# Splitting a GpSimd product in two: one product over an interleaved signed-sine table against two half products over a sine table and a negative-sine table

## The chip, the cores and the metric

One core of one Trainium2 chip runs the program. The metric is the device time of one execution in microseconds (us). Lower is better. Most executions of one kernel agree within 0.3%. Some are slower, and runs over 1.5% above the fastest of the same kernel are called slow and left out of comparisons. Faster or slower needs 2%.

## The reference

```python
# x: (8, 2048, 8, 64) float32; cos, sin: (2048, 32) float32
x1, x2 = x[..., :32], x[..., 32:]
out1 = x1 * cos - x2 * sin
out2 = x1 * sin + x2 * cos
return np.concatenate([out1, out2], axis=-1)      # cos, sin broadcast over batch and head
```

33.5 MB come in and 33.5 MB go out. Per output element there are two products and one sum.

## The kernel before

A batch is one tile of 128 partitions and 8192 elements (4 MB). Five such buffers rotate. Each batch is worked in tiles of mostly 2048 elements (sometimes 1024), in one of three ways: A puts t1 = x times cosine on the vector engine (DVE), t2 = swapped x times signed sine on GpSimd (POOL) and the sum on DVE. B is the same with the sum on the tensor engine and the copy-out on ACT (the scalar engine). C uses no GpSimd. Of the 34 tiles 32 are of kind A or B.

```python
cos_sb = t1s_pool.tile([P, R, Dh], f32, tag="t1s", name="cos_sb")
sin_sb = t1s_pool.tile([P, R, Dh], f32, tag="t1s", name="sin_sb")
sgn = const_pool.tile([P, R, 2, Dh], f32, tag="sg")      # -sin and sin, interleaved
# ... cut ...
for lo, hi in ((0, 4), (4, R)):                          # lines 90 and 91, on ACT
    keep(nc.scalar.mul(sgn[:, lo:hi, 0, :], sin_sb[:, lo:hi, :], -1.0))
    keep(nc.scalar.copy(sgn[:, lo:hi, 1, :], sin_sb[:, lo:hi, :]))
# ... cut: in rotate(), for kinds A and B ...
keep(nc.gpsimd.tensor_mul(                               # line 134
    out=t2.rearrange("p (r h u d) -> p r h u d", r=nr, h=H, u=2),
    in0=swapped(xt, nr),                                 # halves of each head exchanged, negative step
    in1=signed(sgn[:, r0 : r0 + nr, :, :], nr)))
keep(nc.vector.tensor_mul(out=t1..., in0=xk, in1=rep(cos_ps[...], 2 * H)))   # line 141
if kind == "A":
    keep(nc.vector.tensor_add(out=xt, in0=t1, in1=t2))   # line 148
# ... cut: kinds B and C; store() on the ACT queue is line 74, load() on the SP queue line 67 ...
```

Of the kernel before, what the change touches and what calls it, by code (L numbers as in the profile page):

```python
# [9 lines left out]
@with_exitstack  # L10
def kernel(
    ctx: ExitStack,
    tc: tile.TileContext,
    x: bass.AP,
    cos: bass.AP,
    sin: bass.AP,
    out: bass.AP,
):
    nc = tc.nc
    keep = tc.keep_in_program_order  # L20
    f32 = mybir.dt.float32
    PSUM = bass.MemoryType.PSUM

    B, S, H, D = x.shape
    Dh = D // 2
    P = 128
    HD = H * D
    R = S // P
    ROW = R * HD
    UNIT = 4 * HD  # L30
    NBUF = 5
    C = 512
    last = B - 1

    xv = x.rearrange("b (q r) h d -> b q (r h d)", q=P)
    ov = out.rearrange("b (q r) h d -> b q (r h d)", q=P)
    cos_src = cos.rearrange("(q r) d -> q r d", q=P)
    sin_src = sin.rearrange("(q r) d -> q r d", q=P)

    const_pool = ctx.enter_context(tc.tile_pool(name="const", bufs=1))  # L40
    tab_pool = ctx.enter_context(tc.tile_pool(name="tab", bufs=1, space=PSUM))
    t1_pool = ctx.enter_context(tc.tile_pool(name="t1p", bufs=1, space=PSUM))
    o_pool = ctx.enter_context(tc.tile_pool(name="op", bufs=2, space=PSUM))
    t1s_pool = ctx.enter_context(tc.tile_pool(name="t1s", bufs=2))
    xpool = ctx.enter_context(tc.tile_pool(name="xpool", bufs=NBUF))
    t2_pool = ctx.enter_context(tc.tile_pool(name="t2p", bufs=3))

    cos_sb = t1s_pool.tile([P, R, Dh], f32, tag="t1s", name="cos_sb")
    sin_sb = t1s_pool.tile([P, R, Dh], f32, tag="t1s", name="sin_sb")
    sgn = const_pool.tile([P, R, 2, Dh], f32, tag="sg")  # L50
    eye = const_pool.tile([P, P], f32, tag="eye")
    neye = const_pool.tile([P, P], f32, tag="neye")
    cos_ps = tab_pool.tile([P, R, Dh], f32, tag="cp")
    sin_ps = tab_pool.tile([P, R, Dh], f32, tag="sp")

    xts = {}

    def spans(sizes):
        lo = 0
        for n in sizes:  # L60
            yield lo, n
            lo += n

    def load(b):
        xt = xpool.tile([P, ROW], f32, tag="xt", name=f"xt{b}")
        for lo, n in spans([UNIT, UNIT, 2 * UNIT] if b == 0 else [ROW]):
            keep(nc.sync.dma_start(out=xt[:, lo : lo + n], in_=xv[b, :, lo : lo + n]))  # L67
            if b == 0 and lo == 0:
                keep(nc.sync.dma_start(out=cos_sb, in_=cos_src))  # L69
                keep(nc.sync.dma_start(out=sin_sb, in_=sin_src))  # L70
        xts[b] = xt

    def store(b, lo, n):
        keep(nc.scalar.dma_start(out=ov[b, :, lo : lo + n], in_=xts[b][:, lo : lo + n]))  # L74

    for b in range(NBUF):
        load(b)

    nc.gpsimd.memset(eye, 0.0)  # L79
    nc.gpsimd.affine_select(  # L80
        out=eye,
        in_=eye,
        compare_op=mybir.AluOpType.not_equal,
        fill=1.0,
        base=0,
        pattern=[[-1, P]],
        channel_multiplier=1,
    )
    for lo, hi in ((0, 4), (4, R)):
        keep(nc.scalar.mul(sgn[:, lo:hi, 0, :], sin_sb[:, lo:hi, :], -1.0))  # L90
        keep(nc.scalar.copy(sgn[:, lo:hi, 1, :], sin_sb[:, lo:hi, :]))  # L91
    keep(nc.scalar.copy(sin_ps, sin_sb))  # L92
    keep(nc.scalar.mul(neye, eye, -1.0))
    keep(nc.vector.tensor_copy(cos_ps, cos_sb))  # L94

    def rep(a, n):
        return dataclasses.replace(a, ap=[a.ap[0][:], a.ap[1][:], [0, n], a.ap[-1][:]])

    def swapped(a, nr):
        return dataclasses.replace(  # L100
            a,
            offset=a.offset + Dh,
            ap=[a.ap[0][:], [HD, nr], [D, H], [-Dh, 2], [1, Dh]],
        )

    def signed(a, nr):
        return dataclasses.replace(
            a, ap=[a.ap[0][:], [D, nr], [0, H], [Dh, 2], [1, Dh]]
        )

    kinds = {}
    for b, kind in ((1, "C"), (2, "B"), (3, "C"), (4, "B"), (5, "B")):
        kinds[(b, 0)] = kind

    def rotate(b, lo, n):
        kind = kinds.get((b, lo), "A")
        xt = xts[b][:, lo : lo + n]
        r0 = lo // HD
        nr = n // HD
        xk = xt.rearrange("p (r k d) -> p r k d", r=nr, d=Dh)  # L120
        xu = xt.rearrange("p (g u d) -> p g u d", u=2, d=Dh)
        if kind == "A":
            t1 = t1_pool.tile([P, n], f32, tag="t1")
        else:
            t1 = t1s_pool.tile([P, n], f32, tag="t1s")
        if kind == "C":
            t2 = t1s_pool.tile([P, n], f32, tag="t1s")
        else:
            t2 = t2_pool.tile([P, n], f32, tag="t2")
        t1u = t1.rearrange("p (g u d) -> p g u d", u=2, d=Dh)  # L130
        t2u = t2.rearrange("p (g u d) -> p g u d", u=2, d=Dh)
        if kind != "C":
            keep(
                nc.gpsimd.tensor_mul(  # L134
                    out=t2.rearrange("p (r h u d) -> p r h u d", r=nr, h=H, u=2),
                    in0=swapped(xt, nr),
                    in1=signed(sgn[:, r0 : r0 + nr, :, :], nr),
                )
            )
        keep(  # L140
            nc.vector.tensor_mul(  # L141
                out=t1.rearrange("p (r k d) -> p r k d", r=nr, d=Dh),
                in0=xk,
                in1=rep(cos_ps[:, r0 : r0 + nr, :], 2 * H),
            )
        )
        if kind == "A":
            keep(nc.vector.tensor_add(out=xt, in0=t1, in1=t2))  # L148
        elif kind == "B":
            for j in range(n // C):  # L150
                o = o_pool.tile([P, C], f32, tag="o")
                cs = slice(j * C, (j + 1) * C)
                nc.tensor.matmul(o, eye, t1[:, cs], start=True, stop=False)  # L153
                nc.tensor.matmul(o, eye, t2[:, cs], start=False, stop=True)  # L154
                keep(nc.scalar.copy(xt[:, cs], o))  # L155
        else:
            keep(
                nc.vector.tensor_mul(  # L158
                    out=t2.rearrange("p (r k d) -> p r k d", r=nr, d=Dh),
                    in0=xk,  # L160
                    in1=rep(sin_ps[:, r0 : r0 + nr, :], 2 * H),
                )
            )
            G = C // Dh
            for u in range(2):
                for j in range(n // 2 // C):
                    o = o_pool.tile([P, C], f32, tag="o")
                    gs = slice(j * G, (j + 1) * G)
                    nc.tensor.matmul(o, eye, t1u[:, gs, u, :], start=True, stop=False)  # L169
                    nc.tensor.matmul(  # L170
                        o, eye if u else neye, t2u[:, gs, 1 - u, :], start=False, stop=True
                    )
                    keep(
                        nc.scalar.copy(  # L174
                            xu[:, gs, u, :], o.rearrange("p (g d) -> p g d", d=Dh)
                        )
                    )

    def pieces(b):
        if b == 0:  # L180
            return [2 * HD, 2 * HD, UNIT, UNIT, UNIT]
        if b == last:
            return [UNIT, UNIT, UNIT, 2 * HD, 2 * HD]
        return [UNIT] * 4

    def shares(b):
        if b == 0:
            return [HD, 7 * HD, 2 * UNIT]
        if b == last:
            return [2 * UNIT, UNIT, UNIT]  # L190
        return [ROW]

    for b in range(B):
        done = 0
        outs = list(spans(shares(b)))
        for lo, n in spans(pieces(b)):
            rotate(b, lo, n)
            done = lo + n
            while outs and sum(outs[0]) <= done:
                store(b, *outs.pop(0))  # L200
        if b + NBUF <= last:
            load(b + NBUF)
# [30 lines left out]
```

## Time and profile before

| | before |
|---|---|
| median of the first three runs | 163.64 us (163.49 to 164.29) |
| span in the profile | 161.6 us |
| DVE / GpSimd busy | 87% / 84% |
| share of the two DMA queues | 49.7% + 48.3% |

Two rows of the page's slices (tenths of each of 40 slices that the engine was busy) and the row of the chain that ended last, for the kernel before:

```profile
DVE  0458999999999999999999899999999998999900
...
POOL 1199999999999799989995989997999969999100
...
DMA 46%; DVE 36%; POOL 8%; issue 4%; SPq 1%; ACT 0%; DVEq 0%; POOLq 0%; ACTq 0%
```

Three resources look nearly full. The rows cannot say which of them is the bound. GpSimd's sevens, fives and sixes are pauses in which it waits for a load or for a free buffer.

### The profile page before, as it was taken

Reading aid. Unit: us, or ns where it says so; the run is one execution under the profiler, and the core shown is the slowest. Engines: PE = TensorE matmul, PEld = TensorE weight load, DVE = VectorE, ACT = ScalarE, POOL = GpSimd, SP = SyncE. Lnnn points to the kernel's source line nnn. Section 1 sums busy time; section 2 is a strip of 40 time slices with the busy share of each in tenths; the row PEclk is TensorE's granted clock in tenths of the full one; section 3 lists DMA queues with packets and bytes.
Section 4 is the critical chain, followed back from the end, with each engine's and each line's share of the span. In section 5 each row is a group of like instructions: output and inputs, shape, how many; then the busy total and the mean of one; then the engine's idle time right before and its main releaser. Section 6 shows DMA issues by size and latency. Waiting matters only on the chain.

```text
span 161.6 us, 440 instructions
## 1 busy us (share of the span) xinstructions
PE 47.1 (29%) x80; PEld 18.7 (12%) x80; DVE 140.1 (87%) x66; ACT 15.1 (9%) x27; POOL 135.8 (84%) x38
## 2 busy tenths in 40 slices
PE   0000000499008940895029901991000000000000
PEld 0000000134003410331014301340000000000000
DVE  0458999999999999999999899999999998999900
ACT  3310000012100220022001300121000000000000
POOL 1199999999999799989995989997999969999100
PEclk9999999999855898579556995599755555555555
DMA  5999999899999999999999998999999999999994
GB/s 187 418 438 482 463 397 390 373 426 507 397 389 450 426 487 389 446 462 389 446 462 389 462 448 381 487 422 389 487 422 397 479 422 397 479 422 397 430 400 209
DMA packets 3457, 67.64 MB, mean 419 GB/s; under 512 B 384, under 2 KB 384, under 8 KB 768
## 3 DMA queue, kind: packets, MB, share of 16 engines
q1 hardware_dynamic: 1728, 34.08, 49.7%
q10 hardware_dynamic: 1728, 33.56, 48.3%
q14 instruction: 1, 0.01, 0.0%
HBM read 34.08 MB, written 33.55 MB: 419 GB/s over the span
## 4 chain that ended last, share of the span: by engine, by line
DMA 46%; DVE 36%; POOL 8%; issue 4%; SPq 1%; ACT 0%; DVEq 0%; POOLq 0%; ACTq 0%
DMA xt<-in_x_dram 24%; DVE t L141 19%; DMA out_dram<-xt 18%; DVE xt L148 16%; POOL t L134 8%; DMA sin_sb<-in_sin_dram 3%; DVE t L158 1%; SPq L69 0%; SPq L67 0%; ACT sgn L91 0%; DVEq L148 0%; ACT sgn L90 0%; POOLq L134 0%; ACTq L74 0%
## 5 line engine op out<-in xcount | busy, mean ns | idle before, releaser
L134 POOL TENSOR_TENSOR t<-xt,sgn 128x2048 f32<-128x2048 f32 (+1 forms) x32 | 135.1, 4253 | 13.5 <-ACT sgn L91 6.0
L141 DVE TENSOR_TENSOR t<-xt,cos_ps 128x2048 f32<-128x2048 f32 (+1 forms) x34 | 73.4, 2166 | 0.8
L148 DVE TENSOR_TENSOR xt<-t,t 128x2048 f32<-128x2048 f32 (+1 forms) x29 | 62.2, 2144 | 6.3 <-POOL t L134 3.4
L153 PE MATMUL o<-t,eye 128*128 128x512 f32 x24 | 16.1, 759 | 24.7 <-DVE t L141 24.7
L169 PE MATMUL o<-t,eye 128*128 128x512 f32 x16 | 11.8, 844 | 37.6 <-DVE t L141 37.6
L154 PE MATMUL o<-t,eye 128*128 128x512 f32 x24 | 14.9, 709 | 0.0
L155 ACT COPY xt<-o 128x512 f32<-128x512 f32 x12 | 7.0, 586 | 45.0 <-PE o L154 45.0
L153 PEld LDWEIGHTS o<-t,eye 128*128 128x128 f32 x24 | 5.8, 255 | 33.0 <-issue 33.0
L174 ACT COPY xt<-o 128x512 f32<-128x512 f32 x8 | 4.7, 586 | 44.6 <-DVE t L141 26.0
L169 PEld LDWEIGHTS o<-t,eye 128*128 128x128 f32 x16 | 3.8, 256 | 42.5 <-POOL t L134 30.6
L154 PEld LDWEIGHTS o<-t,eye 128*128 128x128 f32 x24 | 5.4, 227 | 7.8 <-issue 7.8
L94 DVE COPY cos_ps<-cos_sb 128x512 f32<-128x512 f32 x1 | 0.7, 694 | 6.1 <-DMA cos_sb<-in_cos_dram 6.1
L170 PE MATMUL o<-t,neye 128*128 128x512 f32 x8 | 5.7, 830 | 0.2 <-DVE t L158 0.2
L158 DVE TENSOR_TENSOR t<-xt,sin_ps 128x2048 f32<-128x2048 f32 x2 | 4.6, 2279 | 0.0
L170 PE MATMUL o<-t,eye 128*128 128x512 f32 x8 | 4.1, 592 | 0.0
L170 PEld LDWEIGHTS o<-t,neye 128*128 128x128 f32 x8 | 2.2, 294 | 4.7 <-issue 4.7
L170 PEld LDWEIGHTS o<-t,eye 128*128 128x128 f32 x8 | 1.5, 190 | 1.9 <-issue 1.9
L90 ACT ACT_TABLE_LOAD x1 | 1.3, 1283 | 0.7 <-PEq L217 0.7
L90 ACT ACTIVATE sgn<-sin_sb 128x128 f32<-128x128 f32 (+1 forms) x2 | 0.8, 413 | 4.8 <-DMA sin_sb<-in_sin_dram 4.8
L91 ACT COPY sgn<-sin_sb 128x128 f32<-128x128 f32 (+1 forms) x2 | 0.8, 388 | 0.0
L92 ACT COPY sin_ps<-sin_sb 128x512 f32<-128x512 f32 x1 | 0.6, 577 | 0.0
L79 POOL MEMSET eye<- 128x128 f32 x1 | 0.2, 206 | 0.3 <-POOLq L217 0.3
(6 smaller groups left out, 1.0 us busy)
## 6 DMA issues: line engine op xcount, KB each, us to landing
xt<-in_x_dram SPq DMA_DIRECT2D x7, 4096.0 KB, 39.1
out_dram<-xt ACTq DMA_DIRECT2D x6, 4096.0 KB, 28.2
out_dram<-xt ACTq DMA_DIRECT2D x2, 2048.0 KB, 19.0
xt<-in_x_dram SPq DMA_DIRECT2D x2, 1024.0 KB, 5.9
xt<-in_x_dram SPq DMA_DIRECT2D x1, 2048.0 KB, 11.4
out_dram<-xt ACTq DMA_DIRECT2D x2, 1024.0 KB, 8.8
out_dram<-xt ACTq DMA_DIRECT2D x1, 1792.0 KB, 20.4
cos_sb<-in_cos_dram SPq DMA_DIRECT2D x1, 256.0 KB, 4.9
```

Source lines behind the costliest of these rows:

```text
L90: keep(nc.scalar.mul(sgn[:, lo:hi, 0, :], sin_sb[:, lo:hi, :], -1.0))
L91: keep(nc.scalar.copy(sgn[:, lo:hi, 1, :], sin_sb[:, lo:hi, :]))
L134: nc.gpsimd.tensor_mul(out=t2.rearrange("p (r h u d) -> p r h u d", r=nr, h=H, u=2), in0=swapped(xt, nr), in1=signed(sgn[:, r0 : r0 + nr, ...
L141: nc.vector.tensor_mul(out=t1.rearrange("p (r k d) -> p r k d", r=nr, d=Dh), in0=xk, in1=rep(cos_ps[:, r0 : r0 + nr, :], 2 * H),)
L148: keep(nc.vector.tensor_add(out=xt, in0=t1, in1=t2))
L153: nc.tensor.matmul(o, eye, t1[:, cs], start=True, stop=False)
L154: nc.tensor.matmul(o, eye, t2[:, cs], start=False, stop=True)
L155: keep(nc.scalar.copy(xt[:, cs], o))
L158: nc.vector.tensor_mul(out=t2.rearrange("p (r k d) -> p r k d", r=nr, d=Dh), in0=xk, in1=rep(sin_ps[:, r0 : r0 + nr, :], 2 * H),)
L169: nc.tensor.matmul(o, eye, t1u[:, gs, u, :], start=True, stop=False)
L170: nc.tensor.matmul(o, eye if u else neye, t2u[:, gs, 1 - u, :], start=False, stop=True)
L174: nc.scalar.copy(xu[:, gs, u, :], o.rearrange("p (g d) -> p g d", d=Dh))
```

## The change

The intent is a simpler access pattern on GpSimd: no swap inside one product and no interleaved table. The first product no longer waits for ACT to build a table, and ACT builds one table in one instruction instead of an interleaved one in four. The price is twice as many GpSimd products.

```diff
-    cos_sb = t1s_pool.tile([P, R, Dh], f32, tag="t1s", name="cos_sb")
-    sin_sb = t1s_pool.tile([P, R, Dh], f32, tag="t1s", name="sin_sb")
-    sgn = const_pool.tile([P, R, 2, Dh], f32, tag="sg")
+    cos_sb = const_pool.tile([P, R, Dh], f32, tag="cb")
+    sin_sb = const_pool.tile([P, R, Dh], f32, tag="sb")
+    nsin = const_pool.tile([P, R, Dh], f32, tag="ns")
 # ... cut ...
-    for lo, hi in ((0, 4), (4, R)):
-        keep(nc.scalar.mul(sgn[:, lo:hi, 0, :], sin_sb[:, lo:hi, :], -1.0))
-        keep(nc.scalar.copy(sgn[:, lo:hi, 1, :], sin_sb[:, lo:hi, :]))
+    keep(nc.scalar.mul(nsin, sin_sb, -1.0))
 # ... cut: the helpers swapped() and signed() go ...
-            keep(
-                nc.gpsimd.tensor_mul(
-                    out=t2.rearrange("p (r h u d) -> p r h u d", r=nr, h=H, u=2),
-                    in0=swapped(xt, nr),
-                    in1=signed(sgn[:, r0 : r0 + nr, :, :], nr),
+            for u, tab in ((1, sin_sb), (0, nsin)):
+                keep(
+                    nc.gpsimd.tensor_mul(
+                        out=t2u[:, :, u, :].rearrange("p (r h) d -> p r h d", h=H),
+                        in0=xu[:, :, 1 - u, :].rearrange("p (r h) d -> p r h d", h=H),
+                        in1=rep(tab[:, r0 : r0 + nr, :], H),
+                    )
                 )
-            )
```

More of the change, by code (lines that the diff above doesn't have):

```diff
@@ L97, in rep @@
         return dataclasses.replace(a, ap=[a.ap[0][:], a.ap[1][:], [0, n], a.ap[-1][:]])
-    def swapped(a, nr):
-        return dataclasses.replace(
-            a,
-            offset=a.offset + Dh,
-            ap=[a.ap[0][:], [HD, nr], [D, H], [-Dh, 2], [1, Dh]],
-        )
-    def signed(a, nr):
-        return dataclasses.replace(
-            a, ap=[a.ap[0][:], [D, nr], [0, H], [Dh, 2], [1, Dh]]
-        )
     kinds = {}
@@ L132, in rotate @@
         if kind != "C":
-            keep(
-                nc.gpsimd.tensor_mul(
-                    out=t2.rearrange("p (r h u d) -> p r h u d", r=nr, h=H, u=2),
-                    in0=swapped(xt, nr),
-                    in1=signed(sgn[:, r0 : r0 + nr, :, :], nr),
+            for u, tab in ((1, sin_sb), (0, nsin)):
[5 more added lines that the diff above has]
+                    )
                 )
-            )
         keep(
```

## The prediction

> **What bounds the kernel now.** I read the page's summary rows and slices first, then the DMA queues, then every store's issue and landing, and only then the engines, because two engines above 80% and a full DMA row cannot all be the bound.
>
> ```profile
> span 161.6 us, 440 instructions
> PE 47.1 (29%) x80; PEld 18.7 (12%) x80; DVE 140.1 (87%) x66; ACT 15.1 (9%) x27; POOL 135.8 (84%) x38
> ...
> DMA  5999999899999999999999998999999999999994
> ...
> DMA packets 3457, 67.64 MB, mean 419 GB/s; under 512 B 384, under 2 KB 384, under 8 KB 768
> ...
> q1 hardware_dynamic: 1728, 34.08, 49.7%
> q10 hardware_dynamic: 1728, 33.56, 48.3%
> ```
>
> The two DMA queues (loads on one, stores on the other) together take 49.7 + 48.3 = 98.0% of sixteen engines' span. Only the first and the last slice of 4 us are not full. DVE is 87% busy and GpSimd (POOL) 84%, but a share of busy time alone does not say which of the three would lengthen the span. For that I took the stores one at a time: when the ACT queue issued each and how long until it landed.
>
> ```profile
> L74 ACTq DMA_DIRECT2D out_dram<-xt x1: 338/338/338, 114.5 to 114.5; - x1
> ...
> DMA to landing us min/median/max: 26.9/26.9/26.9
> ...
> L74 ACTq DMA_DIRECT2D out_dram<-xt x1: 339/339/339, 133.6 to 133.6; - x1
> ...
> DMA to landing us min/median/max: 17.5/17.5/17.5
> ...
> L74 ACTq DMA_DIRECT2D out_dram<-xt x1: 339/339/339, 148.2 to 148.2; - x1
> ...
> DMA to landing us min/median/max: 10.2/10.2/10.2
> ...
> L74 ACTq DMA_DIRECT2D out_dram<-xt x1: 338/338/338, 153.3 to 153.3; - x1
> ...
> DMA to landing us min/median/max: 7.4/7.4/7.4
> ```
>
> The store of batch 5 lands at 114.5 + 26.9 = 141.4, while that of batch 6 was issued at 133.6: it had lain in the queue for 7.8 us already. It lands at 151.1. The last but one store (issued 148.2) lands at 158.4, and the last one, issued at 153.3, 5.1 us before that, lands at 160.7, 2.3 us after its forerunner. For 1 MB that is 1.05 MB / 2.3 us = 455 GB/s, the rate of the busy slices, so the last store is limited by transfer and not by when it was issued. The same subtraction for all twelve stores, from the same view, gives a head start of 6.1, 10.9, 7.0, 10.2, 11, 14, 17, 7.8, 7.7, 7.7 and 5.1 us from the second store on. So the store queue never runs dry after the first store (issued at 11.0), and the loads of batches 5, 6 and 7 are issued 19 to 20 us before their forerunner lands. The bound is the transfer of 67.64 MB. Compute has about 5 us of slack at its tightest place, the last store.
>
> The chain of waits looks different: DMA 46%, DVE 36%, POOL 8%. It follows one last releaser at each step and passes through DVE up to a store's issue at 63.0; a store that then waits 10 us behind another store shows there as part of one long DMA step. I therefore take the queue arithmetic over the chain's shares.
>
> **What the Trainium skill says.** (1) "SBUF — State Buffer", section "SBUF: two separate sides", gives about 436 GB/s as the ceiling of DMA to and from SBUF, 432 measured. The stages of this trace agree: 426 to 445 GB/s between 29 and 149 us. 67.64 MB at 435 would be 155.5 us, and the remaining 6 us are the first and last slices. (2) "GPSIMD Engine Reference", section 3.1, gives 4497 ns for a two-input tensor_tensor of 2048 fp32, about 2.6 cycles an element, against 2293 on the vector engine, and calls it the floor of two operands through one read port. This trace has 4525 and 2291, although the product before reads halves swapped with a negative step. So the awkward pattern costs nothing that a simpler one could give back. (3) "Perfetto Trace Analysis", section "GPSIMD Engine Instruction", advises timing GpSimd by start-to-start spacing and not by the reported duration. The trace supports this: consecutive 2048-element products start at 11.96, 16.43 and 20.89, so 4.47 apart, less than the 4.52 that one reports. (4) "SBUF — State Buffer", section "Who interferes with whom": a vector instruction with two SBUF inputs contends with GpSimd's reads. Here each vector product has its table in PSUM, and each add has t1 in PSUM, so no vector instruction has two SBUF inputs, before or after; the constant 2.29 us in the trace agrees.
>
> **The change part by part.** The profile rows and starts that carry the size of it:
>
> ```profile
> L134 POOL TENSOR_TENSOR t<-xt,sgn 128x2048 f32<-128x2048 f32 x28 | 125.9, 4525 | 7.4 <-DVE xt L148 3.8 <-DMA xt<-in_x_dram 3.7
> ...
> L134 POOL TENSOR_TENSOR t<-xt,sgn 128x1024 f32<-128x1024 f32 x4 | 9.3, 2346 | 6.0 <-ACT sgn L91 6.0
> ```
>
> *The split.* 28 products of 2048 become 56 of 1024, and 4 of 1024 become 8 of 512. The elements stay 32 runs of 32 for each half of a 2048 tile; a half skips every other run. From the starts 7.35, 9.65 and 11.96 a 1024 product has a spacing of 2.305 us; a 2048 product has 4.47. The slope is (4.47 - 2.305) / 1024 = 2.114 ns an element, and the fixed part 2.305 - 1024 x 2.114 ns = 0.14 us. Each split adds one fixed part: 32 x 0.14 = 4.5 us on GpSimd. In reported busy time, 56 x 2.346 = 131.4 and 8 x about 1.26 (2.346 less 512 elements of (4525 - 2346) / 1024 = 2.13 ns) = 10.1, with 0.7 of other work: about 142 against 135.8, or 88% of the span. A tile then costs GpSimd 2 x 2.305 = 4.61 us against the 4.73 that an ordinary tile costs DVE (its products by the cosine in batch 6 start at 119.38, 124.11 and 128.83), so even within a run of ordinary tiles DVE stays the slower of the two.
>
> *The start.* Before, ACT made the first quarter of the signed table in two instructions (6.77 to about 7.3) and GpSimd began at 7.35. After, the first half product reads the loaded sine itself, so it can begin on its landing at 6.75, near 6.85: 0.5 us earlier. Its second half needs the negative sine, one ACT instruction over 512 elements. From 309 ns for 128 and 517 for 384 that is about 0.62 us, ready at 7.4; the first half of 512 elements lasts to about 8.1, so nothing waits. The first tile is ready about 9.35 instead of 9.69, the first store goes out 0.3 us earlier. That adds no bandwidth, since the loads fill the engines then (442 GB/s from 8 to 12).
>
> *The middle.* From tile 3 on, each tile adds 0.14. GpSimd is 0.2 us early at tile 3 (11.73 against 11.96), even at tile 5, and 0.5 late when its first eight tiles end (39.4 against 38.9). Batch 2 landed at 39.2, so it begins about 0.2 late. Then its idle time eats the rest: before batch 4 lands (73.1) it has idled 0.88 + 0.19 + 0.21 on DVE's buffers and 1.05 on the load, 2.3 us, against 0.2 + 7 x 0.14 = 1.2 needed; before batch 6 (112.5) it has 1.68 + 0.60 + 0.22 + 0.88 = 3.4 against 8 x 0.14 = 1.1; before batch 7 (131.85) it has 1.41 against 0.6. At each load's arrival it is back in step.
>
> *The end.* Batch 7 begins at 131.85 as now. Its first t2 is 0.14 later, so DVE's first add begins at 136.5 instead of 136.4. DVE then sets the pace at 4.73 a tile against 4.61, and its last add ends at about 153.4 instead of 153.3. The last store has 5.1 us in hand and loses 0.14 of them.
>
> *Buffers.* The raw tables leave the pool that they shared with t1s, so the first t1s tile at 28.2 waits for no table reader; the last of them (sin_ps) was done at 8.6, so nothing is gained. SBUF per partition grows by 2 KB. The table instructions on ACT drop from four to one, on an engine that is 9% busy.
>
> The sum on the path that sets the end: 0 from the split, 0 from the start, 0 from the buffers. GpSimd gets 4.5 us more work and idles less. The time is that of before.
>
> **The rivals.** *GpSimd becomes the bound.* It would, if each split cost much more than 0.14: GpSimd idles 7.4 us between its first and its last product, and the last store has 5.1, so roughly 12 us, an estimate, or 0.39 us a tile, vanish before the span grows one for one. For it: 84% is near the limit, and the half's stride (64 elements between runs, in input and output) is a pattern that no product of before has. Against it: the old input was in runs of 32 too, and ran at the plain-pattern speed. If the strided writes cost a further 20% (0.9 us a tile), the time would be 32 x (0.14 + 0.9) - 12 = 21 us more, about 185 us.
>
> *The split pays back.* If the five-dimensional swapped pattern hides a penalty, the halves would be quicker and GpSimd would finish earlier. The 4525 ns speaks against it; and were it true, the transfers would still end at the same time: 163.5 us.
>
> *The store queue runs dry once.* If the small delays piled up on a store, the time would grow by the gap. The tightest places are 5.1 us at the end and 6.1 at the second store, which comes when the kernel is still early or even; a delay of 0.5 us reaches neither. This would make 163.7 us at most.
>
> **The range and the chances.** The three runs before spread from 163.49 to 164.29, and I expect that spread and nothing else: 163.6 us, with 163.1 to 164.4 eight times in ten. Faster by over 2% would need less than 160.4 us, under what the bytes at the full rate and the two ends allow: 1%. Slower by over 2% needs 3.3 us, so a split at (12 + 3.3) / 32 = 0.48 us a tile or more, the first rival: 3%. Within 2%: 96%.
>
> **What would show it right or wrong.** The changed page should have GpSimd at 141 to 143 us busy in 70 instructions, half products at about 2.35 us each spaced by 2.30, and fewer waits of GpSimd for DVE and loads in the middle; the DMA row full from slice 2 to 39, with the queues at about 98% together; DVE ending near 153.4 and each store issued within 0.7 us of its old time; GpSimd's first product at about 6.85. I am wrong if half products take over 2.5 us, if DVE's idle time before the adds grows from 6 us to over 12 with GpSimd as the releaser, or if a store lands much less than 5 us after being issued with the queue empty before it.

## The result and the profile after

| | before | changed |
|---|---|---|
| median of 6 runs | 163.58 us (163.43 to 164.29) | 163.37 us (163.27 to 196.16) |
| span in the profile | 161.6 us | 161.4 us |
| GpSimd busy, instructions | 135.8 us, 38 | 139.0 us, 70 |
| first GpSimd product starts | 7.35 us | 7.03 us |
| last sum on DVE ends | 153.32 us | 153.30 us |

The ratio is 0.9982, with a 95% interval from 0.996 to 1.0005: the same. A ratio here is the mean time of one kernel's fast runs over that of the other's of the same rounds, so it is not quite the ratio of the medians. One of the six changed runs took 196.16 us and counts as slow. It was not the profiled one, so nothing of it is known but its length and its granted TensorE clock (1.0, where the others have 0.73 to 0.76).

The page of the changed kernel, the rows that answer to those of before:

```profile
span 161.4 us, 467 instructions
...
PE 46.4 (29%) x80; PEld 18.5 (11%) x80; DVE 140.1 (87%) x66; ACT 14.4 (9%) x24; POOL 139.0 (86%) x70
...
POOL 1299999999999899998996999998999979999200
...
DMA  5999999899999999999999999999999999999995
...
q1 hardware_dynamic: 1728, 34.08, 49.8%
q10 hardware_dynamic: 1728, 33.56, 48.4%
```

GpSimd has 3.2 us more work and the span is 0.2 us shorter. The two queues are busy for the same 98% of the span. The extra work went into GpSimd's pauses, as the groups by shape of the changed kernel show (busy us, mean ns, then the idle time before them and what ended it):

```profile
L121 POOL TENSOR_TENSOR t<-xt,sin_sb 128x1024 f32<-128x1024 f32 x28 | 65.4, 2335 | 5.0 <-DMA xt<-in_x_dram 2.8 <-DVE xt L135 1.8
L121 POOL TENSOR_TENSOR t<-xt,nsin 128x1024 f32<-128x1024 f32 x28 | 65.4, 2335 | 0.0
...
L121 POOL TENSOR_TENSOR t<-xt,sin_sb 128x512 f32<-128x512 f32 x4 | 5.0, 1258 | 5.7 <-DMA sin_sb<-in_sin_dram 5.7
L121 POOL TENSOR_TENSOR t<-xt,nsin 128x512 f32<-128x512 f32 x4 | 5.0, 1257 | 0.0
```

Before, the large products had 7.4 us of idle time in front of them; now the first halves have 5.0 and the second halves none. That is 2.4 of the 3.2 us; the rest is, to a tenth, a start 0.3 us earlier and an end 0.4 us later (the last product ends at 150.31, before at 149.92). The start, in order of time, in the changed kernel (start us, length us):

```profile
7.03 1.27 POOL L121 TENSOR_TENSOR t<-xt,sin_sb 128x512 f32<-128x512 f32 x1 [5.72 <-DMA sin_sb<-in_sin_dram]
8.25 1.25 POOL L121 TENSOR_TENSOR t<-xt,nsin 128x512 f32<-128x512 f32 x1
9.46 1.26 POOL L121 TENSOR_TENSOR t<-xt,sin_sb 128x512 f32<-128x512 f32 x1
10.67 1.26 POOL L121 TENSOR_TENSOR t<-xt,nsin 128x512 f32<-128x512 f32 x1
11.89 2.33 POOL L121 TENSOR_TENSOR t<-xt,sin_sb 128x1024 f32<-128x1024 f32 x1
14.17 2.32 POOL L121 TENSOR_TENSOR t<-xt,nsin 128x1024 f32<-128x1024 f32 x1
16.45 2.32 POOL L121 TENSOR_TENSOR t<-xt,sin_sb 128x1024 f32<-128x1024 f32 x1
```

The first product waits for the sine's landing and not for ACT. Halves of 512 are 1.21 us apart and halves of 1024 are 2.28 apart, so a half costs 0.14 us fixed and (2.28 - 1.21) / 512 = 2.09 ns an element. A 2048 tile takes 4.56 us, against 4.47 before. And the last two stores of the changed kernel (issue, then us to landing):

```profile
L74 ACTq DMA_DIRECT2D out_dram<-xt x1: 339/339/339, 148.1 to 148.1; - x1
...
DMA to landing us min/median/max: 10.0/10.0/10.0
...
L74 ACTq DMA_DIRECT2D out_dram<-xt x1: 338/338/338, 153.3 to 153.3; - x1
...
DMA to landing us min/median/max: 7.3/7.3/7.3
```

They land at 158.2 and 160.6 (by the unrounded times of the trace). The last store still lay in the queue for 4.9 us behind the one before it.

### The profile page after: what moved, and what is told of

The parts are those of the page before. It is cut to its first block, busy times and chain, and to the rows that moved or that the text cites. A ratio compares the mean times of both kernels' runs of the same rounds, so it can differ in the third digit from the quotient of the medians.

```text
span 161.4 us, 467 instructions
## 1 busy us (share of the span) xinstructions
PE 46.4 (29%) x80; PEld 18.5 (11%) x80; DVE 140.1 (87%) x66; ACT 14.4 (9%) x24; POOL 139.0 (86%) x70
## 4 chain that ended last, share of the span: by engine, by line
DMA 46%; DVE 37%; POOL 9%; issue 2%; SPq 1%; DVEq 0%; POOLq 0%; ACTq 0%
DMA xt<-in_x_dram 24%; DVE t L128 18%; DMA out_dram<-xt 18%; DVE xt L135 17%; POOL t L121 9%; DMA sin_sb<-in_sin_dram 3%; DVE t L145 1%; SPq L69 0%; SPq L67 0%; DVEq L135 0%; POOLq L121 0%; ACTq L74 0%
## 5 line engine op out<-in xcount | busy, mean ns | idle before, releaser
L121 POOL TENSOR_TENSOR t<-xt,sin_sb 128x1024 f32<-128x1024 f32 (+1 forms) x32 | 70.4, 2200 | 10.7 <-DMA sin_sb<-in_sin_dram 5.7
L121 POOL TENSOR_TENSOR t<-xt,nsin 128x1024 f32<-128x1024 f32 (+1 forms) x32 | 70.4, 2200 | 0.0
L156 PE MATMUL o<-t,eye 128*128 128x512 f32 x16 | 10.9, 781 | 36.8 <-DVE t L128 36.8
L157 PE MATMUL o<-t,neye 128*128 128x512 f32 x8 | 4.9, 714 | 0.2 <-DVE t L145 0.2
L89 ACT ACTIVATE nsin<-sin_sb 128x512 f32<-128x512 f32 x1 | 0.6, 629 | 4.9 <-DMA sin_sb<-in_sin_dram 4.9
## 6 DMA issues: line engine op xcount, KB each, us to landing
out_dram<-xt ACTq DMA_DIRECT2D x1, 1792.0 KB, 20.4
```

What stands on the lines that cost most here:

```text
L89: keep(nc.scalar.mul(nsin, sin_sb, -1.0))
L121: nc.gpsimd.tensor_mul(out=t2u[:, :, u, :].rearrange("p (r h) d -> p r h d", h=H), in0=xu[:, :, 1 - u, :].rearrange("p (r h) d -> p r h d" ...
L156: nc.tensor.matmul(o, eye, t1u[:, gs, u, :], start=True, stop=False)
L157: nc.tensor.matmul(o, eye if u else neye, t2u[:, gs, 1 - u, :], start=False, stop=True)
```

## The experiments

The theory was that the 67.6 MB of transfers set the time and that GpSimd has some 12 us of pauses and head start to spend. The rivals were that GpSimd's work counts one for one, or that the split pays for itself by a cheaper pattern. Kernels of one group ran on the same chip and share their runs of the kernel before. There are four groups, each on another chip: the first four experiments; the next four, up to the changed kernel again; the split again with the changed kernel beside it; and the last two.

### No rotation at all

```diff
         for lo, n in spans(pieces(b)):
-            rotate(b, lo, n)
             done = lo + n
```

> The changed kernel without any rotation: every batch is loaded and stored as it is (a wrong result on purpose). Theory, that the 67.6 MB of transfers set the time: 161.5 to 163.6 us, at most 1.2% under the kernel before. Rival, that GpSimd or the vector engine are on the path and the full DMA row is partly waiting: under 155 us.

Measured: 163.04 us median (162.73 to 163.09), ratio 0.9955, interval 0.9931 to 0.9979. Its page:

```profile
span 161.3 us, 88 instructions
...
DVE 0.7 (0%) x1; ACT 2.6 (2%) x4; POOL 0.7 (0%) x6
...
DMA  5999999999999999999999999999999999999995
```

With no arithmetic left, only 0.5% is gained. Moving these bytes with this order of loads and stores takes 163 us, and no change to the arithmetic alone, with these transfers kept, can be expected to win more than that.

### No GpSimd products

```diff
         if kind != "C":
-            for u, tab in ((1, sin_sb), (0, nsin)):
-                keep(nc.gpsimd.tensor_mul(...))
+            pass
-            keep(nc.vector.tensor_add(out=xt, in0=t1, in1=t2))
+            keep(nc.vector.tensor_add(out=xt, in0=t1, in1=xt))
-                nc.tensor.matmul(o, eye, t2[:, cs], start=False, stop=True)
+                nc.tensor.matmul(o, eye, t1[:, cs], start=False, stop=True)
```

> The changed kernel without the GpSimd products (the sum takes the input in place of the second product; a wrong result on purpose). GpSimd's 139 us of work are gone. Theory (transfers): 162.5 to 163.7 us, as before. Rival (GpSimd at 84 to 86% is near the bound and holds up the vector engine's sums): 3 to 8 us less, the last sum and the last store earlier by as much.

Measured: 163.44 us (163.38 to 163.51), ratio 0.9984, interval 0.9961 to 1.0006. GpSimd is busy for 0.7 us instead of 139.0 and the time is that of before. GpSimd, as the changed kernel uses it, is not on the path that sets the time.

### Four products a tile

```diff
             for u, tab in ((1, sin_sb), (0, nsin)):
+                step = nr // 2
+                for q in range(0, nr, step):          # each half product in two
```

> Each half product cut once more: four products a tile. With 0.14 us fixed and 2.09 ns an element, a 2048 tile costs GpSimd 4.84 us against 4.56 with halves and 4.47 before; in all 11.9 us more work than before. Theory (about 12 us of idle time and head start to use up): 163.2 to 164.2 us, same. Rival (GpSimd's work counts one for one): 12 us more, about 175 us; half of it: 169 us.

Measured: 163.88 us (163.33 to 163.95), ratio 1.0003, interval 0.9975 to 1.0031. GpSimd is busy for 148.0 us, 12.2 more than before, and there is no effect on the time. In the list of waits of this kernel GpSimd waits for nothing any more after its first product; the wait has changed sides:

```profile
DVE xt L138 <- POOL t L124: 7.9, 15, 1.9
...
POOL t L124 <- DMA sin_sb<-in_sin_dram: 5.8, 1, 5.8
```

(The columns after the colon are us in total, times, and the longest.) The slack is spent, but not overspent.

### Six products a tile

The edits of this run and of the next are shown against the run before each.

```diff
-                step = nr // 2
+                step = nr // 2 if u else 1            # two of 512 and four of 256
```

> Six products a 2048 tile (two of 512 and four of 256): 5.12 us a tile, in all 19.8 us more GpSimd work than before. Theory: the slack of some 12 us is used up, GpSimd runs without a pause from 7 to about 161 us, the last sum ends near 162.5, and the last store, now with no store ahead of it, lands 4.5 to 7 us later: 168 to 171 us, so 5 to 8 us of the 19.8 are seen. Rival (one for one): 183 us. If nothing is seen (163.5 us), the slack is larger than I reckoned.

Measured: 170.85 us (170.83 to 170.86), ratio 1.0436, interval 1.0408 to 1.0464. On its page GpSimd never pauses, and the DMA row breaks for the first time:

```profile
POOL 1399999999999999999999999999999999999930
...
DMA  5999999999999999999999999999999990897846
```

GpSimd runs from 7.07 to 162.2. A 2048 tile takes 5.14 us (successive tiles start at 12.49 and 17.63), and a 1024 tile 2.71. That is 28 x (5.14 - 4.47) + 4 x (2.71 - 2.305) = 20.4 us more than before, of which 170.85 - 163.62 = 7.2 are seen (163.62 is the median of before in these rounds). About 13 us were absorbed, where the prediction estimated 12. The miss in the expectation is the end: the last sum ended at 164.3, not 162.5, and the last store landed 3.9 us after its issue, less than the 4.5 to 7 expected. Nothing lay ahead of it: the store before it had landed at 163.0, 1.3 us before the last one was issued.

### Eight products a tile

```diff
-                step = nr // 2 if u else 1
+                step = 1                              # eight of 256
```

> Eight products of 256 elements a tile. From the six-piece run (two of 512 spaced 1.21, four of 256 spaced 0.68, a tile in 5.13): 8 x 0.68 = 5.42 us a tile, 28 x 0.29 = 8.1 us more GpSimd work than there. Theory: with the slack used up, all further work counts one for one: 170.85 + 8.1 = 179 us (178 to 180). Rival (GpSimd's work is only half on the path, shared with the vector engine): 175 us.

Measured: 178.96 us (178.84 to 179.09), ratio 1.0945, interval 1.0927 to 1.0963. Beyond the slack the work counts one for one: a large tile now takes 5.42 us (successive halves of a tile start at 12.45, 15.16 and 17.86), 28 x 0.28 = 7.8 us more in all, and the time is 8.1 us longer (on another chip, where the kernel before took 163.53). With the kernels of before and after these runs make one curve: GpSimd's work can go from nothing to 148 us without effect, and between six and eight products a tile every further microsecond is paid in full.

### The split alone, over the old table

```diff
-            keep(nc.gpsimd.tensor_mul(
-                    out=t2.rearrange("p (r h u d) -> p r h u d", r=nr, h=H, u=2),
-                    in0=swapped(xt, nr),
-                    in1=signed(sgn[:, r0 : r0 + nr, :, :], nr)))
+            for u in (1, 0):
+                keep(nc.gpsimd.tensor_mul(
+                        out=t2u[:, :, u, :].rearrange("p (r h) d -> p r h d", h=H),
+                        in0=xu[:, :, 1 - u, :].rearrange("p (r h) d -> p r h d", h=H),
+                        in1=rep(sgn[:, r0 : r0 + nr, u, :], H)))
```

> The split alone, over the interleaved signed table of before (two half products; tables, pools and start as before). Expected: first product near 7.35 as before, not 7.03; time 163.2 to 163.9, same. Half products spaced 2.28 if the gain of 1% an element comes from not swapping inside one product; 2.30 to 2.31 if it comes from the dense tables.

Measured: 163.81 to 170.81 us, median 166.03. Two of the six runs, the profiled one among them, count as slow. The fast ones have the ratio 1.0091, interval 1.0043 to 1.014, which is under the 2% but clear of 1. This was not expected. GpSimd's first product began at 7.58, not near 7.35 as expected. GpSimd was not the cause: a whole batch 7 takes it 18.57 us in this kernel and 18.59 in the changed one. It waited for loads instead. The trace has 16 completion signals for each transfer, as many as the core has DMA engines. I take each to be the signal of one engine, which the trace does not say; then the time from the first to the last of them says how far the engines are apart. In the kernel before it was 0.4 to 1.1 us. Here it grew from 0.8 us at the landing of batch 1 to 9.5 at the landing of batch 7. Since this was a slow run, it proved nothing by itself.

### One product without the swap

```diff
-                    in0=swapped(xt, nr),
+                    in0=xt.rearrange("p (r h u d) -> p r h u d", r=nr, h=H, u=2),
```

> The kernel before with one product a tile that reads the input in its own order, without the swap of halves (a wrong result on purpose). If the swap with its negative step costs the 1% an element: 2048 products spaced 4.42 us. If not: 4.47. Time 163.3 to 163.9 either way.

Measured, one look: 163.48 us, of unknown state. Three 2048 products in a row take 13.45 us and the last of them 4.51, so they are (13.45 - 4.51) / 2 = 4.47 apart, as before. The swap costs nothing. The 1% an element that the halves gain comes neither from the lack of a swap nor, by the run above (18.57 us), from the dense tables. Where it comes from stays open. It amounts to 0.05 us a tile.

### The changed kernel again

There is no edit.

> The changed kernel once more, five rounds, since one of its six runs took 196 us. If that was a chance state, none or one of these is slow and the fast ones are at 163.3 to 163.6; if it belongs to the kernel, about one in six is at 190 or more.

Measured: 163.31 to 164.00 us, median 163.96, ratio 1.0019, interval 1.0003 to 1.0034. No run was slow. The fast runs reach a little higher than I expected. Of the kernel before one of twelve runs in this group was slow, at 167.12. What the 196.16 us of the first series was stays open: it came once in the sixteen runs of the changed kernel.

### The split alone, again, beside the changed kernel

There is no edit.

> The split alone once more. In its first run the 16 completions of one transfer lay up to 9.5 us apart, against 0.4 to 1.1 in the kernel before, while GpSimd's products were as quick as in the changed kernel and GpSimd waited for loads. If that was a chance state of some DMA engines: 163.2 to 164.0 us now, completions under 2 us apart. If it belongs to this kernel: again 164 to 171 us with wide spreads, and then the tables or pools of the full change are what avoids it.

> The changed kernel as a measure beside it on the same chip: 163.2 to 164.1 us, completions of one transfer under 2 us apart.

Measured for the split alone: 163.61 to 166.25 us, median 164.99, ratio of the fast runs 1.0066, interval 1.0016 to 1.0116. Five of the six are fast (163.61 to 165.94); the sixth, at 166.25, counts as slow, as does one of the kernel before here, at 166.30. For the changed kernel: 163.26 to 163.35 us, median 163.30, ratio 0.9979, interval 0.996 to 0.9999. So the fast runs of the split alone are 0.7 to 0.9% slower on two chips, which by the 2% rule still counts as the same. Scatter is not its alone: in the last three groups 3 of 34 runs of the kernel before are slow, against 3 of 12 of the split alone. But 4 of its 9 fast runs lie above 164.5 us, and none of the 44 fast runs of the kernel before does. Now both profiles are of fast runs and may be compared. The waits of GpSimd for loads, first the split alone:

```profile
POOL t L135 <- DMA xt<-in_x_dram: 5.2, 4, 1.7
```

and the changed kernel, in its first profile:

```profile
POOL t L121 <- DMA xt<-in_x_dram: 2.8, 3, 1.1
```

And where GpSimd begins batch 7, again the split alone first:

```profile
134.20 18.59 POOL L135 TENSOR_TENSOR t<-xt,sgn 128x1024 f32<-128x1024 f32 x10 [1.00 <-DMA xt<-in_x_dram]
```

```profile
131.71 2.34 POOL L121 TENSOR_TENSOR t<-xt,sin_sb 128x1024 f32<-128x1024 f32 x1 [1.08 <-DMA xt<-in_x_dram]
```

The same load comes 2.5 us later. I took the spread of the 16 completions from the trace:

```
us from the first to the last of the 16 completions; landing time of the load in brackets
load of batch          4             5             6             7        last store
before             0.4 ( 73.0)   0.4 ( 92.4)   1.1 (112.4)   1.1 (131.7)     1.0
changed            0.5 ( 73.1)   0.6 ( 92.4)   1.0 (112.2)   1.0 (131.6)     0.9
changed, again     0.5 ( 73.0)   0.5 ( 92.3)   1.6 (112.9)   1.6 (132.2)     1.5
unswapped          1.8 ( 73.1)   1.8 ( 92.5)   2.2 (112.3)   2.1 (131.7)     0.9
split alone, again 2.7 ( 73.8)   4.3 ( 94.8)   4.4 (114.5)   4.6 (134.1)     3.2
split, early first 0.5 ( 73.0)   0.5 ( 92.3)   1.2 (112.4)   1.2 (131.8)     1.1
changed, late first 0.6 ( 71.6)  0.8 ( 91.2)   1.8 (111.7)   2.1 (131.5)     2.1
```

In all these rows the first completion of the last store comes at 159.7 to 160.0 us; what differs is the last one, from 160.6 (changed) to 163.2 (split alone, again), and the span goes with it, from 161.4 to 164.0. If each signal is one engine's, engines out of step lengthen the end without moving a byte more. What differs early on is the moment of the first store: 11.0 in the kernel before, 10.8 to 10.9 in the changed one, 11.3 to 11.4 with the split alone, which has the late start of the old table and the longer first tile of the split. The last two runs try this.

### The split alone, with an early first product

```diff
-                        in1=rep(sgn[:, r0 : r0 + nr, u, :], H),
+                        in1=rep(sin_sb[:, r0 : r0 + nr, :] if u and b == 0 and lo == 0
+                                else sgn[:, r0 : r0 + nr, u, :], H),
```

> The split over the interleaved table, but the very first half product reads the raw sine, so that GpSimd begins near 7.05 and the first store is issued near 10.9 as in the changed kernel (11.3 to 11.4 with the split alone). If the moment of the first store is what puts the 16 DMA engines out of step: 163.2 to 163.8 us, completions of one transfer under 2 us apart. If the tables and pools do it: again 164 to 170 us and 3 to 9 us apart.

Measured: 163.34 us (163.29 to 163.45), all fast, ratio 0.9978, interval 0.996 to 0.9995. One operand of one product out of 64 was exchanged. GpSimd started at 7.06 and the first store went out at 10.8:

```profile
7.06 1.26 POOL L135 TENSOR_TENSOR t<-xt,sin_sb 128x512 f32<-128x512 f32 x1 [5.75 <-DMA sin_sb<-in_sin_dram]
```

The spread is back to 0.5 to 1.2 us. The old table and the old pools are all still there, so they are not enough to cause it. This run was on another chip than the two of the split alone; each is compared with the kernel before on its own chip.

### The changed kernel with a late first store

```diff
             for u, tab in ((1, sin_sb), (0, nsin)):
+                # ... cut: in the first tile of batch 0 alone, eight products of 128 elements ...
```

> The changed kernel with the first tile's product cut in eight, so that the first store is issued near 11.6 instead of 10.8; GpSimd has 0.9 us more work in all. If the moment of the first store matters: 164 us or more, completions 3 us or more apart. If not: 163.2 to 163.9 us, under 2 us apart.

Measured: 164.43 us (163.88 to 165.62), all fast, ratio 1.0047, interval 1.0012 to 1.0083. The first store went out at 11.7. The time is where the theory of the moment puts it, but the spread reached 2.1 us, not 3. So an early start of GpSimd takes the loss of the split away, and a late one brings a smaller loss to the changed kernel. That the moment of the first store is what matters is argued and not shown: the same edits also move GpSimd's own work and the second store (18.8 to 19.0 in the early kernels, 19.3 to 19.7 in the late ones). Nor does lateness alone say how much: the kernel with four products a tile issued its first two stores at 11.2 and 19.8, had spreads up to 2.1 us and was as fast as before; the one without the swap issued its first at 11.1 and had up to 2.2. By what mechanism the engines fall out of step, and which of them lag, the traces do not show.

## Why the prediction was right

- **The bound.** The prediction took the queue arithmetic over the shares of busy time and over the chain. The run without arithmetic (0.9955) and the one without GpSimd products (0.9984) show that this was right. The 436 GB/s that the prediction cites is not a hard ceiling here: four of the seven stages between 29 and 149 us lie at 437 to 445.
- **The head start of the stores.** By the unrounded times the last store's head start was 4.97 us before and 4.86 after; the prediction's 5.1 came from rounded lines, as did its 2.3 us between the last two landings (2.43, so 432 GB/s and not 455). Nothing hangs on either. The last sum ended at 153.30 (predicted 153.4).
- **The slack of about 12 us.** It was an estimate from the pauses and the last store. Six products a tile measured about 13, and four products sat at its edge.
- **The size of the split.** The fixed part of 0.14 us was right. The elements were 1% quicker than assumed, so the split costs 0.09 us a large tile and 3.2 us in all, not 0.14 and 4.5. The predicted busy time of about 142 us was too high also because it added up reported durations, and consecutive products overlap by some 0.05 us: those of the half products add up to 140.8 us, where the page counts overlaps once and has 139.0 with 0.7 of other work in it. The prediction had itself cited the advice to use the spacing.
- **The start.** 0.5 us was predicted for the first product and 0.3 us for the first store; it became 0.32 and 0.2. In this execution the sine landed at 6.89 instead of 6.75, and GpSimd began 0.14 after that.
- **The sum of zeros.** It came out as predicted, but two of its terms were not zero. "0 from the split, 0 from the start" was argued from bandwidth. The split alone, with the old start, costs 0.7 to 0.9%, with the completions of a transfer further apart, and the earlier start takes this back. That the two cancelled is luck: the prediction foresaw neither. Both are under 2%, so its forecast of no change beyond 2% did not need the luck; its closeness to 163.6 did.
- **The rivals.** GpSimd became the bound only where it was given 20 us of extra work or more. The pattern gave back 0.05 us a tile, too little to see. The store queue did not run dry in the changed kernel. With six products it did: its last store landed 3.9 us after being issued, against 7.3.

## What to carry to other kernels

Subtract each transfer's issue from its forerunner's landing: this head start, together with the pauses of the suspected engine, tells how much work that engine can take before the span grows, and it was right here to about 1 us. An engine that is 86% busy can be entirely off the path. Where the transfers set the time, half a microsecond at the start can matter more than extra work later: here the same 64 half products cost 0.7 to 0.9% with the late start and nothing with the early one. So test the parts of a change one at a time even when the whole shows nothing, and look at how far apart the completions of one transfer lie.

## What the Trainium skill lacked or had wrong

- "DMA: Bandwidth & Descriptors", section "Latency and other measured facts", says that some engines (7 and 15) are usually slower in traces and guesses at software-generated descriptors as the cause. All big transfers here are issued from the SP and ACT queues, and the completions of one transfer still lay up to 4.6 us apart in a fast run (9.5 in a slow one). The page does not say that the start of a kernel can bear on this: the split alone went from a ratio of 1.0066 to 0.9978 (on two chips) when GpSimd's first product moved from 7.5 to 7.1 us and its first store from 11.3 to 10.8. Which engines lag was not seen, so nothing here speaks for or against 7 and 15.
- "GPSIMD Engine Reference", section 3.1, gives 4497 ns and about 2.6 cycles an element for a two-input add of 2048. It names the dispatch of an instruction as a cost but gives no time for it on GpSimd; section 2.1 puts one part of it, an indirect call, at tens of cycles. The spacings of the products here give 0.14 us fixed and 2.09 to 2.11 ns an element.
